# Matrix operands of a hybrid decoder layer moved by 64 bytes within on-chip memory

## The chip, the cores and the metric

The kernel runs on one core of one Trainium2 chip. The metric is device time in microseconds (us); lower is better. Three runs of the kernel before took 2049.73, 2051.74 and 2052.04 us, a median of 2051.74 us. The engines' names in the profile are PE (matrix multiplication; PEld is its separate row for loading weights), DVE (vector), ACT (scalar, with its activation functions), POOL and SP; the last two mostly start transfers.

## The reference

One decoder layer over 512 positions of width 2048, in float32. What matters here is its matrix products:

```python
proj = einsum('bsd,de->bse', h, w_in)          # 2048 -> 5120: q, k, v, xr, xg
o_attn = stick_breaking_attention(q, k, v)     # 8 heads of 128
hr = rg_lru(causal_depthwise_conv(xr), ...)    # gated linear recurrence, 1024 wide
mixed = concat([rmsnorm(o_attn), rmsnorm(hr * gelu(xg))])
x = x + gt1 * einsum('bse,ed->bsd', mixed, w_out)       # 2048 -> 2048
hid = square(relu(einsum('bsd,df->bsf', h2, w_mlp_in))) # 2048 -> 8192
x = x + gt2 * einsum('bsf,fd->bsd', hid, w_mlp_out)     # 8192 -> 2048
```

Each sub-layer's input is normalised and then scaled and shifted by vectors that come from `c @ w_ada` (2048 -> 12288); the result is normalised once more.

## The kernel before, in words

Everything is kept transposed: 128 features on the partitions, positions along the row. A float32 operand is split into a high part of the format `float32r` and a low part that holds the rest, and each product is three matmuls: high weights times high data, high weights times low data, low weights times high data (`mm3`, lines 258 to 263, and lines 1099 to 1101). In a matmul the *weights* (128 x 128, 512 bytes of a partition) are loaded into PE by an instruction of their own, LDWEIGHTS, and the *moving operand* (256 or 512 columns, 1024 or 2048 bytes of a partition) is streamed past them.

- Up to about 670 us: the products with `w_in` and most of those with `w_out`. They are matmuls of 512 columns. The weights arrive by transfer in a tile `wr`, ACT copies the high part to `wh` (line 244) and DVE subtracts to get the low part `wl` (line 122). For the value projection (`v_mm`, lines 470 to 472) the roles are changed: the data are the weights, and 256 columns of `wh` and `wl` are the moving operand. The first product, up to 110 us, keeps its split weights in tiles `a`. Attention, the recurrence and the modulation vectors run beside these as background work, fed in by lanes that are advanced step by step (`tick`).
- From about 670 us to the end: the rest of `w_out` and the two MLP products, all with matmuls of 256 columns. The MLP is a Strassen-Winograd scheme: one step (`strassen`, 1080) is seven products of three matmuls, for two halves, so 42 matmuls. Its weights are combined by `operands` (lines 1050 to 1073): tiles `raw` and `ts`, split into `w3`, `w4` and, for every fifth one, `w5`. The moving operands, data of the first product and the squared hidden layer of the second, are in tiles `a`.

The order of the instructions on each engine comes from a scheduler that goes by priorities; the change touches neither priorities nor instructions.

What matters for the change is where tiles lie within a partition. There are two stacks. The left one grows upward; it holds small constants, then a tile `pad` that nothing reads, and after it `cb` (2 x 4096 bytes), `n` (5 x 2048), `a` (64 x 2048), and on top a stage: first `front` (`wr`, `wh`, `wl`, 2048 bytes each), later in the same place `mlp` (`w5`, 4096, and `w3`, 6 x 3072). The right one grows downward from the end of the memory; it holds a few vectors that fill 512 bytes, then the stage `rows` (`x`, `tt`) and later `sums` (`ts`, `raw`, `w4`). All of these sizes are multiples of 512 bytes, except the constants and the pad:

```python
const(PAD, "pad")
cb = [T("cb"), T("cb")]
for tag in ("n", "a"):
    new(tag)
stage("rows")
stage("front")
```

The constants end at byte 19808 of a partition. With a pad of 40 columns of 4 bytes, `cb` begins at 19968 = 39 x 512, so everything after it begins at 0 modulo 512. The end of the memory, 229376, is 448 x 512, so the tiles on the right are at 0 modulo 512 as well. A moving operand or a block of weights starts at a multiple of 512 bytes within its tile, so before the change both operands of every matmul that counts are at 0 modulo 512 bytes.

Of the kernel before, what the change touches and what calls it, by code (L numbers as in the profile page):

```python
# [40 lines left out]

URGENT = 150
EVAC = 88
PAD = 40

BUFS = {"cb": 2, "a": 64, "ga": 4, "n": 5}
COLS = {
    "wr": 512, "wh": 512, "wl": 512, "x": 1024, "cb": 1024, "tt": 1280, "n": 512, "a": 512, "ga": 4,  # L50
    "raw": 1024, "ts": 1024, "w3": 768, "w4": 1024, "w5": 1024,
}
STAGES = {
    "front": ("left", {"wr": 4, "wh": 3, "wl": 3}),
    "rows": ("right", {"x": 4, "tt": 4}),
    "sums": ("right", {"ts": 2, "raw": 3, "w4": 4}),
    "mlp": ("left", {"w5": 1, "w3": 6}),
}
BANKS = ["mm"] * 4 + ["z"] * 3 + ["o"]
BANKS2 = ["o"] + ["z"] * 3 + ["mm"] * 4  # L60
# [4 lines left out]
def hybrid_layer_kernel(  # L65
# [32 lines left out]
    def T(tag, dt=F32, cols=None):  # L98
        return new(next(split_tag) if tag == "w4" else tag, dt, cols)

    def new(tag, dt=F32, cols=None):
        count[0] += 1
        pool, bufs = (sp, BUFS[tag]) if tag in BUFS else pools[tag][:2]
        return pool.tile([P, cols or COLS[tag]], dt, tag=tag, name=f"{tag}_{count[0]}", bufs=bufs)
# [5 lines left out]
    def const(cols, name, dt=F32):  # L110
        return sp.tile([P, cols], dt, tag=name, name=name)
# [27 lines left out]
    new("ga")  # L139
    const(PAD, "pad")  # L140
    cb = [T("cb"), T("cb")]
# [1318 lines left out]
```

## Time and profile before

| | |
|---|---|
| median of three runs | 2051.74 us |
| the profiled execution's own time, and its span | 2051.77 us, 2050.1 us |
| PE busy | 2009.6 us, 14532 matmuls |
| weight loads (PEld) busy | 1904.8 us, 14532 loads |
| DVE busy | 1764.0 us |
| ACT busy | 1077.8 us |
| POOL busy | 181.0 us |
| transfers | 441.45 MB, 215 GB/s over the span |

The rows of the profile name an engine, a line of the code, what is written and read (`ps_mm<-a,w`: a result bank from tiles `a` and `w3`, `w4` or `w5`, whose numbers are left out) and the shape. The ends of matmuls are modelled and overlap the next one, so what a matmul costs in a row of them is read from the distance between two starts, which the text calls the pitch, and not from its duration.

### The profile page before, as it was taken

To read this page: it belongs to the slowest core of one execution; us is meant where nothing else is said; L and a number is where in the kernel's file an instruction comes from. 1 tells how busy PE (TensorE), PEld (TensorE's weight loads), DVE (VectorE), ACT (ScalarE), POOL (GpSimd) and SP (SyncE) were. 2 spreads that over 40 slices of the span, in tenths; PEclk is the share of its full clock that TensorE was granted. 3 is DMA by queue.
4 is the path that set the end of the run, shared out by engine and by line. 5 is a ranking of instruction groups with operands and counts; after the bars stand their busy time and mean duration, and the time that the engine had idled before them with its cause. 6 is when DMAs were issued, how large, how long until landed. Compare 5 with 4: busy or idle time off the path is not lost.

```text
span 2050.1 us, 37927 instructions
## 1 busy us (share of the span) xinstructions
PE 2009.6 (98%) x14532; PEld 1904.8 (93%) x14532; DVE 1764.0 (86%) x2971; ACT 1077.8 (53%) x1572; POOL 181.0 (9%) x283
## 2 busy tenths in 40 slices
PE   8999999999999998999999999999999999999997
PEld 6789898778887998999999999999999999999996
DVE  8998776978888699999999999999788778778986
ACT  5443655796423575555555555456455555545542
POOL 0000000000000001221121112100011110210000
PEclk9999999999999999999999999999999999999998
DMA  9896646556789444675566656655485576667644
GB/s 363 303 326 201 200 153 203 167 172 206 226 300 325 134 156 149 213 238 182 185 217 198 194 188 220 211 191 176 148 308 207 210 254 235 232 241 248 237 148 149
DMA packets 205624, 441.45 MB, mean 215 GB/s; under 512 B 20353, under 2 KB 41985, under 8 KB 205442
## 3 DMA queue, kind: packets, MB, share of 16 engines
q1 hardware_dynamic: 178642, 360.78, 53.7%
q0 software_dynamic: 21760, 71.32, 8.9%
q10 hardware_dynamic: 5040, 6.93, 1.0%
q8 instruction: 114, 1.87, 0.4%
q14 instruction: 68, 0.56, 0.1%
HBM read 375.25 MB, written 63.70 MB: 214 GB/s over the span
## 4 chain that ended last, share of the span: by engine, by line
PE 57%; DVE 2%; DMA 1%; issue 0%; ACT 0%; SPq 0%; DVEq 0%
PE ps_mm L1101 9%; PE ps_mm L1100 9%; PE ps_mm L1099 9%; PE ps_z L1101 7%; PE ps_z L1100 7%; PE ps_z L1099 7%; PE ps_o L1101 2%; PE ps_o L1099 2%; PE ps_o L1100 2%; DMA raw<-in_w_mlp_out_dram 1%; DMA a<-x 0%; DVE w L122 0%; DMA a<-sum 0%; DVE a L1346 0%; DVE a L1276 0%
## 5 line engine op out<-in xcount | busy, mean ns | idle before, releaser
L1101 PE MATMUL ps_mm<-a,w 128*128 128x256 f32 x1696 | 479.6, 283 | 1.1 <-DVE w L122 1.1
L1100 PE MATMUL ps_mm<-a,w 128*128 128x256 f32 x1696 | 479.8, 283 | 0.0
L1099 PE MATMUL ps_mm<-a,w 128*128 128x256 f32 x1696 | 479.2, 283 | 0.0
L1063 ACT ACTIVATE w<-raw 128x768 fp32r<-128x768 f32 x244 | 204.9, 840 | 379.0 <-PE ps_mm L1100 165.6
L122 DVE TENSOR_TENSOR w<-ts,w 128x1024 fp32r<-128x1024 f32 x244 | 298.0, 1221 | 116.9 <-PE ps_mm L1100 61.6
L1101 PE MATMUL ps_z<-a,w 128*128 128x256 f32 x1304 | 369.5, 284 | 6.2 <-DVE w L122 6.2
L1099 PE MATMUL ps_z<-a,w 128*128 128x256 f32 x1304 | 369.3, 284 | 0.0
L1100 PE MATMUL ps_z<-a,w 128*128 128x256 f32 x1304 | 369.2, 284 | 0.0
L1101 PEld LDWEIGHTS ps_mm<-a,w 128*128 128x128 f32 x1696 | 325.5, 192 | 1.4 <-DVE w L122 1.4
L1100 PEld LDWEIGHTS ps_mm<-a,w 128*128 128x128 f32 x1696 | 325.7, 192 | 0.2 <-DVE a L122 0.2
L1099 PEld LDWEIGHTS ps_mm<-a,w 128*128 128x128 f32 x1696 | 325.5, 192 | 0.1
L1069 ACT ACTIVATE w<-ts 128x1024 fp32r<-128x1024 f32 x244 | 258.2, 1058 | 113.4 <-DVE ts L1065 101.9
L122 DVE TENSOR_TENSOR w<-raw,w 128x768 fp32r<-128x768 f32 (+1 forms) x296 | 267.4, 904 | 34.3 <-ACT w L244 23.4
L1101 PEld LDWEIGHTS ps_z<-a,w 128*128 128x128 f32 x1304 | 250.6, 192 | 7.1 <-DVE w L122 7.0
L1099 PEld LDWEIGHTS ps_z<-a,w 128*128 128x128 f32 x1304 | 250.8, 192 | 0.1
L1100 PEld LDWEIGHTS ps_z<-a,w 128*128 128x128 f32 x1304 | 250.7, 192 | 0.1
L244 ACT ACTIVATE wh<-wr 128x512 fp32r<-128x512 f32 (+1 forms) x184 | 113.0, 618 | 152.2 <-PE ps_mm L262 65.8
L259 PE MATMUL ps_mm<-a,wh 128*128 128x512 f32 x448 | 176.2, 393 | 3.1 <-ACT wh L244 1.4
L263 PE MATMUL ps_mm<-a,wl 128*128 128x512 f32 x448 | 175.1, 391 | 0.4 <-DVE wl L122 0.2
L262 PE MATMUL ps_mm<-a,wh 128*128 128x512 f32 x448 | 174.7, 390 | 0.0
L1057 DVE TENSOR_TENSOR ts<-raw 128x512 f32<-128x512 f32 x244 | 166.6, 683 | 3.5 <-DMA raw<-in_w_mlp_out_dram 2.4
L122 DVE TENSOR_TENSOR wl<-wr,wh 128x512 fp32r<-128x512 f32 (+1 forms) x184 | 123.7, 675 | 33.3 <-ACT wh L244 32.8
(332 smaller groups left out, 4167.0 us busy)
## 6 DMA issues: line engine op xcount, KB each, us to landing
raw<-in_w_mlp_out_dram SPq DMA_DIRECT2D x124, 512.0 KB, 4.0
raw<-in_w_mlp_in_dram SPq DMA_DIRECT2D x120, 512.0 KB, 3.9
x<-in_w_adaT_dram SPq DMA_DIRECT2D x108, 512.0 KB, 5.7
wr<-in_w_in_dram SPq DMA_DIRECT2D x160, 256.0 KB, 3.4
tt<-in_w_adaT_dram SPq DMA_DIRECT2D x52, 512.0 KB, 6.5
part<-a POOLq DMA_DIRECT2D x84, 256.0 KB, 3.9
a<-part SPq DMA_DIRECT2D x84, 256.0 KB, 6.0
prod<-a POOLq DMA_DIRECT2D x63, 256.0 KB, 5.9
```

Source lines behind the costliest of these rows:

```text
L122: tt(out=out, in0=full, in1=f32(high), op=ALU.subtract)
L244: act(h[:, :n], r[:, :n], AF.Copy)
L259: first = mm(out, wh, ah, start=start, stop=False, **kw)
L262: mm(out, wh, al, start=False, stop=False, **kw)
L263: mm(out, wl, ah, start=False, stop=stop, **kw)
L1057: tt(out=t[:, : 2 * HT].rearrange("p (a b) -> p a b", a=2), in0=r[:, HT : 3 * HT].rearrange("p (a b) -> p a b", a=2), in1=r[:, q_(0)].unsq ...
L1063: act(h, r[:, HT:], AF.Copy)
L1069: act(h, t, AF.Copy)
L1099: mm(out, wh[:, blk(i)], ah, start=st, stop=False, **kw)
L1100: mm(out, wh[:, blk(i)], al, start=False, stop=False, **kw)
L1101: mm(out, wl[:, blk(i)], ah, start=False, stop=j == js[-1], **kw)
```

## The change

The pad becomes 16 columns (64 bytes) smaller, and a tile of 64 bytes is put in front of the stage `mlp`:

```diff
-PAD = 40
+PAD, SHIFT = 24, 16
...
-    "raw": 1024, "ts": 1024, "w3": 768, "w4": 1024, "w5": 1024,
+    "raw": 1024, "ts": 1024, "w3": 768, "w4": 1024, "w5": 1024, "shift": SHIFT,
 }
 STAGES = {
     "front": ("left", {"wr": 4, "wh": 3, "wl": 3}),
     "rows": ("right", {"x": 4, "tt": 4}),
     "sums": ("right", {"ts": 2, "raw": 3, "w4": 4}),
-    "mlp": ("left", {"w5": 1, "w3": 6}),
+    "mlp": ("left", {"shift": 1, "w5": 1, "w3": 6}),
```

`cb`, `n`, `a`, `wr`, `wh` and `wl` now begin 64 bytes lower, at 448 modulo 512. `w5` and `w3` are where they were, and so is everything on the right (`x`, `tt`, `ts`, `raw`, `w4`): 0 modulo 512. So the matmuls of 512 columns have both operands at 448, the matmuls of 256 columns from 670 us on have the moving operand at 448 and the weights at 0, and `v_mm` has both at 448. No instruction is added, removed or changed but for these addresses.

## The prediction

> **What bounds the kernel now.** I read the page's first two parts, then the table by stage, then the groups of matmuls, then single starts in the timeline. The top of the page:
>
> ```profile
> span 2050.1 us, 37927 instructions
> PE 2009.6 (98%) x14532; PEld 1904.8 (93%) x14532; DVE 1764.0 (86%) x2971; ACT 1077.8 (53%) x1572; POOL 181.0 (9%) x283
> PEclk9999999999999999999999999999999999999998
> DMA  9896646556789444675566656655485576667644
> ```
>
> PE works 98% of the span at the full granted clock, so the kernel is as long as its matmuls take. Whether another engine would take over at once is read from the table by stage (PE, PEld, DVE, ACT, POOL, then clock, DMA share and GB/s):
>
> ```profile
> 0.00:110.00 110.00, 98.16 (x401) 77.58 (x402) 100.35 (x192) 51.89 (x86) 5.59 (x9) 0.98 0.92 337
> 110.00:260.00 150.00, 149.26 (x884) 132.83 (x883) 128.30 (x212) 71.59 (x114) 0.00 (x0) 1.00 0.69 231
> 671.00:800.00 129.00, 123.47 (x1002) 122.19 (x1001) 108.31 (x219) 83.16 (x162) 7.74 (x14) 0.99 0.44 136
> 800.00:1300.00 500.00, 499.00 (x4155) 498.56 (x4154) 476.26 (x820) 265.63 (x349) 86.36 (x127) 1.00 0.63 205
> 1390.00:2000.00 610.00, 608.50 (x5060) 607.54 (x5060) 498.80 (x746) 314.91 (x415) 60.64 (x112) 1.00 0.63 219
> ```
>
> From 800 to 1300 us DVE is busy for 476 of 500 us, so PE could gain there at most 24 us before DVE bounds it; from 1390 to 2000 us DVE has 111 us of room. The first 110 us hang on transfers and DVE, not on PE.
>
> **What a matmul costs now.** Of 256 columns, and of 512 (starts in the left column):
>
> ```profile
> 1099.75 0.28 PE L1099 MATMUL ps_mm<-a,w 128*128 128x256 f32 x1
> ...
> 1100.95 0.28 PE L1100 MATMUL ps_mm<-a,w 128*128 128x256 f32 x1
> 549.71 0.39 PE L259 MATMUL ps_mm<-a,wh 128*128 128x512 f32 x1
> ...
> 550.84 0.39 PE L263 MATMUL ps_mm<-a,wl 128*128 128x512 f32 x1
> ```
>
> Ten pitches of the first in 1.20 us make 0.120 us; five of the second in 1.13 us make 0.226 us. In one place the clock was granted at half:
>
> ```profile
> 390.52:392.93 2.41, 2.40 (x10) 0.56 0.72 232
> 392.93:393.89 0.96, 0.96 (x4) 0.50 0.48 169
> 392.83 0.31 PE L652 MATMUL ps_z<-tt,nones_r 128*128 128x128 f32 x1
> 392.94 0.73 PE L259 MATMUL ps_z<-a,a 128*128 128x512 f32 x1
> 393.47 0.63 PE L262 MATMUL ps_z<-a,a 128*128 128x512 f32 x1
> 393.90 0.54 PE L263 MATMUL ps_z<-a,a 128*128 128x512 f32 x1
> ```
>
> There 512 columns took 0.43 us (the last two starts) and 128 columns 0.11, a quarter: in proportion, with nothing on top. So at full clock the columns alone are 0.43/2 = 0.215 us for 512 and 0.107 for 256, and what is paid on top is 0.226 - 0.215 = 0.011 and 0.120 - 0.107 = 0.013 us: about the same for both sizes, once per matmul, and absent at half clock. A fixed number of PE's own cycles would have doubled there. So it looks like a time that the streamed operand loses while the next weights are read beside it. That is the one place in which addresses can count: two readers of one memory, whose start addresses are now equal modulo 512 everywhere.
>
> Two more readings say how much that loss can move. After a stall, when the load of weights and the stream stand otherwise to one another, the pitch is another for some matmuls, at the same addresses:
>
> ```profile
> 1380.48 0.28 PE L1100 MATMUL ps_z<-a,w 128*128 128x256 f32 x1
> ...
> 1381.43 0.28 PE L1099 MATMUL ps_z<-a,w 128*128 128x256 f32 x1
> 1941.81 0.28 PE L1099 MATMUL ps_o<-a,w 128*128 128x256 f32 x1
> ...
> 1942.74 0.28 PE L1101 MATMUL ps_z<-a,w 128*128 128x256 f32 x1
> 112.76 0.40 PE L259 MATMUL ps_mm<-a,wh 128*128 128x512 f32 x1
> ...
> 113.92 0.39 PE L263 MATMUL ps_mm<-a,wl 128*128 128x512 f32 x1
> ```
>
> Eight pitches of 256 columns took 0.95 us in the one place and 0.93 in the other: 0.1175 on the mean, 2 to 3 ns under the settled 0.120. Five pitches of 512 columns took 1.16: 0.232, 6 ns over the settled 0.226. So phase matters; the settled phase is a good one for 512 columns and a poor one for 256. The floor is set by the loads themselves; one behind the other, with no stream beside the first, they follow at 0.11 us:
>
> ```profile
> 1380.26 0.19 PEld L1099 LDWEIGHTS ps_z<-a,w 128*128 128x128 f32 x1
> 1380.37 0.19 PEld L1100 LDWEIGHTS ps_z<-a,w 128*128 128x128 f32 x1
> ```
>
> **The change part by part.** It adds and removes no instruction. The matmuls that it touches, by group (the groups of the other two lines of each product have the same counts):
>
> ```profile
> L1101 PE MATMUL ps_mm<-a,w 128*128 128x256 f32 x1696 | 479.6, 283 | 1.1 <-DVE w L122 1.1
> L1101 PE MATMUL ps_z<-a,w 128*128 128x256 f32 x1304 | 369.5, 284 | 6.2 <-DVE w L122 6.2
> L1101 PE MATMUL ps_o<-a,w 128*128 128x256 f32 x416 | 118.0, 284 | 0.4 <-DVE w L122 0.4
> L259 PE MATMUL ps_mm<-a,w 128*128 128x256 f32 x168 | 48.3, 287 | 0.7 <-DVE a L1324 0.4 <-ACT w L244 0.3
> L259 PE MATMUL ps_z<-a,w 128*128 128x256 f32 x92 | 26.2, 285 | 0.0
> L259 PE MATMUL ps_o<-a,w 128*128 128x256 f32 x44 | 12.6, 287 | 0.0
> L470 PE MATMUL ps_mm<-wh,a 128*128 128x256 f32 x128 | 36.5, 285 | 0.3 <-DVE a L460 0.3
> L259 PE MATMUL ps_mm<-a,wh 128*128 128x512 f32 x448 | 176.2, 393 | 3.1 <-ACT wh L244 1.4 <-DVE a L460 1.1 <-DVE a L481 0.6
> ```
>
> *256 columns, stream at 448, weights at 0.* (1696 + 1304 + 416) x 3 = 10248 in the MLP and (168 + 92 + 44) x 3 = 912 beside it: 11160 matmuls. Only here does the distance between the operands change, by 64 bytes. That is 16 columns, 16 x 0.107/256 = 6.7 ns of the stream: as large as the shifts that the stalls made (2 to 6 ns of pitch). No row shows this pair of addresses. Bounds: below, 0.111 us, the floor of the loads; above, the 6 ns by which 512 columns stand worse after a stall, 0.126. I take the nearest row, the pitch of 256 columns out of its settled phase, 0.118 (0.1175, rounded towards no gain): 11160 x 0.002 = 22 us less. DVE's cover holds: from 800 to 1300 us the 4155 matmuls give 8 us, and DVE's 476 us fit into 492.
>
> *512 columns, both at 448.* The distance stays zero, and the phase of the load against the stream with it. The settled 0.226 is the lowest that I see, so 0; bounds -0.002 and +0.006 for some 2200 matmuls, -4 to +13 us.
>
> *v_mm, both at 448*, some 770 matmuls: the distance stays; 0, with bounds of 2 ns each way, 1.5 us. In attention's last product the weights move and the stream (`tt`) does not, in the recurrence's gates too: under 150 matmuls, less than 1 us either way.
>
> *Vector and scalar work on moved tiles.* The convolution reads and writes at offsets of 4, 8 and 12 bytes:
>
> ```profile
> L554 DVE SCALAR_TENSOR_TENSOR a<-a,vec,a 128x510 f32<-128x510 f32 x8 | 5.9, 741 | 0.0
> L717 DVE SCALAR_TENSOR_TENSOR a<-a,vec,n 128x512 f32<-128x512 f32 x16 | 11.6, 742 | 0.0
> ```
>
> 741 ns at an odd offset, 742 without: 0 for DVE. ACT has no such pair of rows; 0 by the same, and with 315 of 610 us it has room for any small loss.
>
> *Transfers into `a`, `n` and `wr`.* No row shows one that starts off 512 bytes. Where they count is the first 110 us, at a DMA share of 0.92:
>
> ```profile
> wr<-in_w_in_dram SPq DMA_DIRECT2D x160, 256.0 KB, 3.4
> a<-in_xT_dram SPq DMA_DIRECT2D x16, 256.0 KB, 6.4
> ```
>
> Of these, 32 + 16 of 256 KB come there, 12.6 MB of the 37 MB that 337 GB/s make in 110 us. If they took a tenth longer, 0.34 x 0.1 x 110 = 4 us; it is zero if the addresses don't matter to a transfer. I take 0.5 us, near zero, since DVE is busy for 100 of the 110 us too. Later the share is 0.63 and loads run ahead: nothing. The Trainium skill (DMA: Bandwidth & Descriptors, "How a descriptor splits into AXI transactions") says that a transaction starts at a multiple of 256 bytes and that a descriptor starting elsewhere pays for bytes that it doesn't use; a row of 2048 bytes from 192 modulo 256 would by my estimate take 70 beats where it took 64, 9% more. It speaks against the change; no run yet shows it.
>
> *The tile of 64 bytes.* Each tile of `mlp` now lies over one tile of `front` more, so its first writer waits for one more old reader. That happens once, around 650 us, when eight blocks of weights in `w4` go first: 0.5 us, bounds 0 and 3.
>
> Sum: -22 + 0.5 + 0.5 = -21 us. The profiled execution's own time is 2051.77 us, the median of the runs 2051.74, the same within 0.03: 2031 us.
>
> **The rivals.**
>
> *Much faster.* The new distance takes the loss away altogether: 0.111 us per matmul of 256 columns. For it: at half clock the loss is nil, so it is no part of PE's own work. Against it: even the best phases after a stall lose most of it. Time: 5060 x 9 ns = 46 us from 1390 to 2000, 1002 x 9 = 9 from 671 to 800, DVE's 24 (not 37) from 800 to 1300, and 8 for the rest: 87 less, 1965 us.
>
> *No change.* The loss is the same at every address. While 512 bytes of weights are read, the stream runs through 1024, so it passes the weights' position once modulo 512 wherever it starts; what it loses in passing might not depend on where. For it: in all of the MLP, where tiles lie at many addresses, the pitch is 0.120, so nothing above 512 bytes matters. Against it: the pitches after stalls. Time: 2052 us.
> The Trainium skill (TensorE: Matmul & The Clock Gate, "Step-by-step: what each phase is for") also leads there: PE has two independent read ports, and loading weights takes nothing from the running matmul, so no address could matter. By its section "Back-to-back issue gap", 256 columns would take 256/2.4 + 2.5 = 109 ns; the trace has 120, so it disagrees in size, and the rule stays only a rival.
>
> *Slower.* The distance of 64 bytes puts stream and load into a worse settled phase, in the same 11160 matmuls. For it: 512 columns lose 6 ns more after a stall, so worse phases exist, and nothing in the trace says on which side this one lies. Against it: for 256 columns the phases seen are on the whole better than the settled one. Half of that price, 0.123, gives 11160 x 0.0028 = 31 us more, 2083 us; the whole, 0.126, gives 2118. It is slower from any settled pitch above 0.1204, the 4 us that a measurement of this kernel can tell from none (0.2%).
>
> **How the numbers follow.** Two of three places after a stall are better phases for their size, and they are the ones with 256 columns; so a better pitch is the likeliest. Chances: forecast 0.33, with its own range 2015 to 2047; much faster 0.20 (1960 to 2015); no change 0.20; slower 0.27 (2056 to 2118). Faster 0.53, same 0.20, slower 0.27. The range leaves out about 1 in 10 at each end, half of the much faster case and a third of the slower one: 1985 to 2085 us.
>
> **What would show it.** Right: about 850 matmuls in 100 us from 1100 us on, where 500 us now hold 4155; the pitch of 512 columns still 0.226; DVE at 97% from 800 to 1300. Wrong: a pitch of 256 columns at or over 0.120; a pitch of 512 columns that moves, which would mean that addresses count by themselves and not by their distance; or transfers into `wr` that land later than 3.4 us.

## The result and the profile after

The changed kernel took 2021.41 us (median of four runs, 2020.68 to 2022.22) where the kernel before took 2050.73: a ratio of 0.9858, interval 0.9841 to 0.9876. It is 29 us faster; the forecast was 2031. That these four agree so well seems to be chance: the same kernel, run again, took from 2014.53 to 2034.26 us (experiment 6, which also says why).

The profiled execution took 2022.22 us, with this page and this table by stage (PE, PEld, DVE, ACT, POOL, clock, DMA share, GB/s):

```profile
span 2020.5 us, 37927 instructions
PE 1967.8 (97%) x14532; PEld 1857.3 (92%) x14532; DVE 1761.0 (87%) x2971; ACT 1076.0 (53%) x1572; POOL 181.1 (9%) x283
0.00:110.00 110.00, 98.15 (x398) 77.58 (x399) 99.72 (x192) 52.37 (x85) 5.70 (x9) 0.98 0.92 336
671.00:800.00 129.00, 121.12 (x998) 118.68 (x996) 108.26 (x219) 82.99 (x162) 7.40 (x13) 0.97 0.43 133
800.00:1300.00 500.00, 496.35 (x4313) 494.08 (x4314) 491.13 (x847) 275.92 (x366) 91.34 (x135) 1.00 0.65 211
1390.00:2000.00 610.00, 604.82 (x5129) 601.74 (x5128) 498.89 (x755) 315.41 (x424) 60.63 (x112) 1.00 0.63 221
```

The first 110 us are as before, and nothing is gained from 671 to 800. From 800 to 1300 us PE starts 4313 matmuls where it started 4155, and DVE has gone from 476 to 491 busy of 500 us. From 1390 to 2000 us there are 5129 instead of 5060, but that window now takes in part of the kernel's end, where PE has little to do. From 1400 to 1850 us, before and after:

```profile
1400.00:1850.00 450.00, 450.00 (x3750) 449.83 (x3748) 358.19 (x527) 229.35 (x300) 53.01 (x98) 1.00 0.64 227
1400.00:1850.00 450.00, 450.00 (x3823) 450.00 (x3822) 362.84 (x533) 232.23 (x302) 52.64 (x98) 1.00 0.66 233
```

These are 73 more in 450 us, about half of the gain per microsecond of the stage before. Starts in the timeline tell the two stages apart, the first product of the MLP and the second:

```profile
999.78 0.28 PE L1101 MATMUL ps_mm<-a,w 128*128 128x256 f32 x1
...
1000.68 0.28 PE L1100 MATMUL ps_o<-a,w 128*128 128x256 f32 x1
1599.77 0.28 PE L1099 MATMUL ps_mm<-a,w 128*128 128x256 f32 x1
...
1600.71 0.28 PE L1101 MATMUL ps_mm<-a,w 128*128 128x256 f32 x1
```

Eight pitches took 0.90 us in the first place and 0.94 in the second: about 0.113 and 0.118. Over long unbroken stretches the two are 0.1133 and 0.1178: the same instruction on the same addresses settles at one of two pitches, and stays there until PE next stalls. Counted over the starts of the 11160 matmuls of 256 columns (the MLP's 10248 and the 912 beside it), 5429 pitches were of 115 ns or less and 5590 of 116 to 125 ns, 4088 of these in one unbroken stretch from 1400 to 1882 us. Before, every settled stretch stood at 0.1200.

Where PE waited from 800 to 1380 us, before and after (us in total, times, longest):

```profile
PE ps_z L1101 <- DVE w L122: 0.6, 1, 0.6
PE ps_o L1101 <- DVE w L122: 0.4, 1, 0.4
```

```profile
PE ps_z L1099 <- ACT a L1110: 1.5, 1, 1.5
PE ps_z L1099 <- DVE a L1115: 1.1, 2, 0.6
PE ps_mm L1099 <- DVE a L1111: 1.1, 1, 1.1
PE ps_z L1101 <- DVE w L122: 0.8, 2, 0.6
```

The first is the whole of that view before, 1 us; after, these four and five smaller ones make 6 us. So the quicker PE now waits in this stage, most often for DVE; experiment 11 tests that it is DVE. The starts show more than this view: taking every pitch above 125 ns among the 11160 matmuls as a stall, what the stalls hold beyond 0.120 us each went from 16.3 to 33.5 us. Of that, 2.2 became 12.4 us between 800 and 1400 us, 8.8 became 13.3 before 800 us, which takes back what the pitch gained there, and 5.2 became 7.9 after 1400 us.

### The profile page after: what moved, and what is told of

The parts are those of the page before. It is cut to its first block, busy times and chain, and to the rows that moved or that the text cites. A ratio compares the mean times of both kernels' runs of the same rounds, so it can differ in the third digit from the quotient of the medians.

```text
span 2020.5 us, 37927 instructions
## 1 busy us (share of the span) xinstructions
PE 1967.8 (97%) x14532; PEld 1857.3 (92%) x14532; DVE 1761.0 (87%) x2971; ACT 1076.0 (53%) x1572; POOL 181.1 (9%) x283
## 5 line engine op out<-in xcount | busy, mean ns | idle before, releaser
L1101 PE MATMUL ps_mm<-a,w 128*128 128x256 f32 x1696 | 472.4, 279 | 1.6 <-DVE w L122 1.6
L1099 PE MATMUL ps_mm<-a,w 128*128 128x256 f32 x1696 | 472.0, 279 | 1.9 <-DVE a L1111 1.1
L1100 PE MATMUL ps_mm<-a,w 128*128 128x256 f32 x1696 | 472.3, 279 | 0.2 <-DVE a L122 0.2
L1101 PE MATMUL ps_z<-a,w 128*128 128x256 f32 x1304 | 364.8, 280 | 7.5 <-DVE w L122 7.5
L1099 PE MATMUL ps_z<-a,w 128*128 128x256 f32 x1304 | 364.6, 280 | 3.1 <-ACT a L1110 1.5
L1100 PE MATMUL ps_z<-a,w 128*128 128x256 f32 x1304 | 364.0, 279 | 0.1
L1099 PEld LDWEIGHTS ps_mm<-a,w 128*128 128x128 f32 x1696 | 321.5, 190 | 2.5 <-issue 2.0
L1101 PEld LDWEIGHTS ps_mm<-a,w 128*128 128x128 f32 x1696 | 318.8, 188 | 2.1 <-DVE w L122 2.0
L1100 PEld LDWEIGHTS ps_mm<-a,w 128*128 128x128 f32 x1696 | 318.6, 188 | 0.6 <-DVE a L122 0.6
L1101 PEld LDWEIGHTS ps_z<-a,w 128*128 128x128 f32 x1304 | 246.0, 189 | 9.2 <-DVE w L122 9.1
L1099 PEld LDWEIGHTS ps_z<-a,w 128*128 128x128 f32 x1304 | 248.0, 190 | 4.5 <-ACT a L1110 1.7
L1100 PEld LDWEIGHTS ps_z<-a,w 128*128 128x128 f32 x1304 | 245.7, 188 | 0.6 <-DVE a L122 0.6
L211 DVE SCALAR_TENSOR_TENSOR x<-x,cb 128x1024 f32<-128x1024 f32 x108 | 131.1, 1217 | 29.5 <-DMA x<-in_w_adaT_dram 29.3
```

Source lines behind the costliest of these rows:

```text
L211: ins = stt(out=t, in0=t, scalar=1.0, in1=cb[q_], op0=ALU.mult, op1=ALU.mult, accum_out=self.ga[:, q_ : q_ + 1],)
L1099: mm(out, wh[:, blk(i)], ah, start=st, stop=False, **kw)
L1100: mm(out, wh[:, blk(i)], al, start=False, stop=False, **kw)
L1101: mm(out, wl[:, blk(i)], ah, start=False, stop=j == js[-1], **kw)
```

## The experiments

Theory: the distance between the two operands' addresses sets the pitch. Rivals: the moving operand's own address sets it; or the wait before a run of matmuls does, and the addresses little. The second question became why the time of one kernel varies, and the third what DVE takes back.

**1. micro.** PE alone: sets of 36 and 24 matmuls of the same kind and order, moving operand and weights at chosen offsets, each set begun after a wait of varied length. It computes nothing of the layer.

```diff
+for rep in range(4):
+    for m, w in N256:          # offsets in bytes, (moving, weights)
+        run(256, m, w, 36, rep)
```

> Not the layer: only PE is measured. Sets of 36 matmuls of 256 columns (24 of 512) in the order of the layer's triples, a short wait between sets, each set with other start addresses modulo 512 (moving operand, weights); four rounds with waits of other lengths (three for 512). Theory 1, the distance of the two operands counts: (0,0), (64,64), (256,256) and (448,448) all settle at 0.120 us; (448,0) and (0,64) both settle at 0.1133 or 0.1178, as in the changed kernel; 512 columns settle at 0.2267 for (0,0) and (448,448), and at another pitch for (448,0). Theory 2, the moving operand's own address counts: (448,448) goes with (448,0), and (0,64) with (0,0). No theory says which other distance is best; the floor of the loads, 0.111, bounds them.

Merged rows of the timeline: pitch is the duration less one matmul's 0.28 us (0.39 for 512 columns), over the count less one. In this order: (0, 0), (448, 448), (448, 0), (0, 64), (64, 0), and for 512 columns (0, 0) and (448, 0).

```profile
118.39 1.72 PE L67 MATMUL b<-mv,wt 128*128 128x256 f32 x13
188.68 1.60 PE L67 MATMUL b<-mv,wt 128*128 128x256 f32 x12
173.83 1.64 PE L67 MATMUL b<-mv,wt 128*128 128x256 f32 x13
203.82 1.75 PE L67 MATMUL b<-mv,wt 128*128 128x256 f32 x14
133.24 1.81 PE L67 MATMUL b<-mv,wt 128*128 128x256 f32 x14
483.78 1.75 PE L67 MATMUL b<-mv,wt 128*128 128x512 f32 x7
527.65 1.79 PE L67 MATMUL b<-mv,wt 128*128 128x512 f32 x7
```

The first is 1.44/12 = 0.120, the second 1.32/11 = 0.120, the third 1.36/12 = 0.1133, the fourth 1.47/13 = 0.113, the fifth 1.53/13 = 0.118. Equal offsets gave 0.120 wherever both lay (0, 64, 256, 448), and so did (256, 0) and (0, 256), and for 512 columns 64, 128 and 192 gave the pitches of 320, 384 and 448: the pattern repeats after 256 bytes. (0, 64), with nothing at 448 but the same distance, gave 0.1133 in three of four rounds and 0.1178 in one. For 512 columns distance 0 is the best, 1.36/6 = 0.2267, and (448, 0) worse, 1.40/6 = 0.2333. So the theory stands against the moving operand's own address. One pair of addresses can take either of two pitches, in rounds that differ in the wait before a set.

**2. all448.** The whole right stack 64 bytes lower as well, so nearly every operand is at 448.

```diff
-    "mlp": ("left", {"w5": 1, "w3": 6}),      # as before, but with PAD = 24
+    top.tile([P, SHIFT], F32, tag="rshift", name="rshift")   # on the right, 64 bytes
```

> The changed kernel with the weights of the 256-column matmuls at 448 too (no tile before w5 and w3, and the right stack 64 bytes lower), so both operands of nearly every matmul are moved by the same 64 bytes. Theory 1, the distance counts: the pitch of 256 columns is 0.120 again, 836 matmuls from 1100 to 1200 us, and the time that of before, 2051 us within 4. Theory 2, the moving operand's own address counts: the pitch stays at 0.113 to 0.118 and the time at 2021 us.

2052.42 us (2050.30 to 2055.14, ten runs), ratio 1.0009, interval 1.0000 to 1.0019. The windows 800 to 1300 and 1400 to 1850 us:

```profile
800.00:1300.00 500.00, 499.53 (x4161) 499.29 (x4161) 477.15 (x821) 266.58 (x350) 86.57 (x127) 1.00 0.64 205
1400.00:1850.00 450.00, 450.00 (x3749) 449.85 (x3748) 357.94 (x527) 229.78 (x300) 53.15 (x98) 1.00 0.64 227
```

4161 matmuls against 4155 before: 448 by itself is worth nothing. The gain is the distance.

**3. front0.** The 64-byte tile ahead of the stage `front`: for matmuls of 512 columns the weights are at 0 and the moving operand at 448.

```diff
-    "front": ("left", {"wr": 4, "wh": 3, "wl": 3}),
+    "front": ("left", {"shift": 1, "wr": 4, "wh": 3, "wl": 3}),
```

> The changed kernel with wr, wh and wl back at 0 (a tile of 64 bytes before them as well), so that the 512-column matmuls have their moving operand at 448 and their weights at 0, but for the first product. Theory 1, the distance counts: their pitch leaves 0.2267 us; the gates, the only ones of 512 columns whose distance the change did alter (64 the other way), went up to 0.232, so slower is likelier: 1800 matmuls by 0 to 6 ns, 2021 to 2032 us. Theory 2, the moving operand's own address counts: as after, 2021 us.

2027.32 us, from 2018.08, 2019.40, 2035.31 and 2035.24; ratio 0.9886, interval 0.9841 to 0.9932. First the changed kernel's row, then that of this one:

```profile
500.00:600.00 100.00, 99.54 (x438) 81.83 (x437) 93.50 (x164) 44.68 (x74) 4.74 (x2) 1.00 0.73 238
```

```profile
500.00:600.00 100.00, 100.00 (x428) 80.05 (x427) 92.97 (x162) 44.08 (x73) 4.14 (x1) 1.00 0.72 234
800.00:1300.00 500.00, 497.60 (x4223) 495.59 (x4221) 483.76 (x830) 272.73 (x360) 88.17 (x129) 1.00 0.64 206
1400.00:1850.00 450.00, 449.83 (x3965) 449.40 (x3964) 377.67 (x557) 240.52 (x316) 53.13 (x98) 1.00 0.67 237
```

The distance does make 512 columns slower, 428 against 438 in 100 us (by their starts 0.2333 against 0.2267 us). But from 110 to 672 us PE waited some 4 us less for other engines, and `v_mm`, whose operands are now 64 bytes apart, went from 0.120 to 0.118. The MLP's first matmul starts at 767.2 us where it started at 765.2, and in experiment 6 the unchanged kernel starts it at 767.2 as well, so no loss in all can be told. The times fall into two pairs 17 us apart. The profiled run (2018.08) has its two MLP stages the other way round from the changed kernel's: 450/3965 = 0.1135 in the second and 500/4223 = 0.118 in the first. 4088 matmuls times 4.4 ns, the two pitches' difference, are 18 us. So the pairs fit a second stage that fell into the one pitch or the other; no run of the slower pair was profiled.

**4. gt2_after.** The changed kernel with less vector work in the MLP's first stage: 64 products of the last modulation vector cover 8 of their 512 columns. It leaves out the rest of that vector. The same cut serves in 8, 9 and 11.

```diff
-                out=t, in0=t, scalar=1.0, in1=cb[q // 2][:, q % 2 * S : (q % 2 + 1) * S], ...
+                out=t[:, :8], in0=t[:, :8], scalar=1.0, in1=cb[q // 2][:, q % 2 * S : q % 2 * S + 8], ...
```

> The changed kernel, with the 64 vector products for the last modulation vector done on 8 of their 512 columns (the rest is left out; transfers and order stay): DVE has some 33 us less to do between 850 and 1400 us. Theory: in that stretch DVE, busy for 491 of 500 us, has become the bound, and the stalls that PE now has there go away: 8 to 18 us faster than after, 2003 to 2013 us. Rival: the stalls come from transfers or from the choice of settled pitch alone: 2021 us within 4.

2012.12 us, from 2012.76, 2011.47, 2033.19 and 2008.24; ratio 0.9840, interval 0.9779 to 0.9902. Its profiled run had 4230 matmuls from 800 to 1300 us, so the stage stood at 0.118; experiment 6 had 4219 there at the same pitch and with all of the vector work, so at 0.118 the cut is worth little. For the time as a whole the run is inconclusive: the draw of the pitch hides the effect.

**5. micro2.** As micro, with every distance in steps of 8 bytes and eight rounds. It computes nothing of the layer.

```diff
-N256 = [(m, 0) for m in (0, 16, 32, 64, 96, 128, 192, ...)] + ...
+N256 = [(m, 0) for m in range(0, 256, 8)] + [(0, w) for w in (16, 32, 48, 64, 80)]
```

> Only PE is measured, as in micro: sets of 27 matmuls of 256 columns (18 of 512), now at every distance of 8 bytes from 0 to 248 (16 for 512), since micro showed that what holds at 64, 128 or 192 holds 256 bytes on as well; eight rounds with waits of other lengths between the sets. Five sets have the distance on the weights' side. Theory: which of two settled pitches a set falls into (0.1133 or 0.1178 at 448, as in the changed kernel) is decided by the wait before it, so a distance of 192 shows both among eight rounds, and the weights at 64 likewise. Open, and what this run is for: whether some distance settles at 0.1133 or lower in all eight rounds, which would give a kernel that doesn't depend on it. Rival: the pitch hangs on the distance alone, and the two values in the kernel come from something else (other engines, transfers): then each distance has one pitch in all eight rounds.

(192, 0) in two rounds, (112, 0), (240, 0) and (0, 16):

```profile
259.42 1.58 PE L65 MATMUL b<-mv,wt 128*128 128x256 f32 x12
998.96 1.64 PE L65 MATMUL b<-mv,wt 128*128 128x256 f32 x13
219.54 1.64 PE L65 MATMUL b<-mv,wt 128*128 128x256 f32 x13
283.24 1.68 PE L65 MATMUL b<-mv,wt 128*128 128x256 f32 x13
291.17 1.71 PE L65 MATMUL b<-mv,wt 128*128 128x256 f32 x13
```

The first two rows are one pair of addresses: 1.30/11 = 0.118 and 1.36/12 = 0.1133, the higher in seven rounds, the lower in one. (112, 0) stood at 0.1133 in all eight. The last two have the same distance and differ, 1.40/12 = 0.1167 and 1.43/12 = 0.119. Their pitches go round in a short cycle, which these rows cut off; over whole cycles the starts give 0.1171 and 0.1183 in every round. So below 32 bytes the distance isn't everything. For 512 columns (0, 0) settled at 0.2267 in both rounds, (240, 0) ran at 0.2267 in one round and 0.2333 in the other, and the rest lay from 0.229 to 0.234, some of them with two pitches as well.

**6. after_again.** The changed kernel once more, unchanged.

> The changed kernel itself, once more. Theory: from 1400 to 1880 us no wait interrupts the matmuls, and the wait before 1400 decides by a hair whether those 4088 settle at 0.1133 or 0.1178 us, so its times fall into two groups 18 us apart, or all into one of them: 2021 or 2003 us. Rival, the pitch is fixed by the kernel: all its times at 2021 us within 2.

2026.69 us, from 2034.26, 2024.20, 2014.53 and 2029.17; ratio 0.9876, interval 0.9848 to 0.9904. The profiled run, the slowest:

```profile
800.00:1300.00 500.00, 497.39 (x4219) 495.60 (x4219) 483.72 (x828) 272.21 (x360) 87.87 (x129) 1.00 0.64 206
1400.00:1850.00 450.00, 450.00 (x3819) 449.67 (x3818) 364.37 (x537) 234.30 (x306) 53.00 (x98) 1.00 0.66 233
```

500/4219 and 450/3819 are both 0.118, where the first profiled run had its first stage mostly at 0.1133. Instead of the two groups that I expected, the times spread over 20 us: the first stage is a draw too. The ratio of the result holds for its four runs; this kernel's time is 2014 to 2034 us.

**7. d112.** A distance of 112 bytes through the weights: moving operand at 384, MLP weights 16 bytes higher.

```diff
-PAD, SHIFT = 24, 16
+PAD, SHIFT = 8, 32
+BY = 16          # added to the addresses of w3, w4, w5 and three small vectors
```

> The changed kernel with the moving operand of 256 columns 112 bytes ahead of the weights modulo 256 (cb, n, a, wr, wh, wl at 384, the weights in w3, w4, w5 at 16 modulo 512; the mask of attention moves into the stage front to make room), a distance at which all eight sets measured alone settled at 0.1133 us. Theory: all of the MLP settles at 0.1133; from 1400 to 1880 us that is 4088 x 4.4 ns = 18 us less than after, and some 900 matmuls between 800 and 1300 us give 4 less what DVE takes back there: 1998 to 2005 us, and the times agree among themselves. Rival: in the layer, with other engines at work, this distance has two settled pitches as well: two groups of times, or 2021 us.

2051.20 us (2042.55 to 2053.54, twelve runs), ratio 0.9999, interval 0.9989 to 1.0009.

```profile
800.00:1300.00 500.00, 499.29 (x4154) 498.60 (x4153) 476.29 (x818) 266.03 (x348) 87.90 (x129) 1.00 0.63 204
1400.00:1850.00 450.00, 450.00 (x3799) 449.80 (x3799) 363.40 (x536) 233.78 (x307) 53.00 (x98) 1.00 0.65 229
```

0.120 in the first stage, 0.1185 in the second: the expectation failed. The distance is micro2's, but there the odd 16 bytes were the moving operand's, here the weights'. The theory, that the distance alone counts, held wherever both offsets were multiples of 64 bytes, and falls with an odd 16.

**8. d112_gt2.** The same with the cut of experiment 4.

> d112 with the 64 vector products for the last modulation vector done on 8 of 512 columns (the rest left out), some 33 us less work for DVE between 850 and 1400 us. With one settled pitch, this tells what DVE costs there. Theory: at 0.1133 us the matmuls of that stretch need 472 us for what took 500, DVE needs 476, so DVE is the bound in parts of it: 5 to 12 us faster than d112. Rival: the stalls come from transfers or waits at the ends of the groups: within 3 us of d112.

2043.94 us (2034.12 to 2055.00, ten runs), ratio 0.9977, interval 0.9957 to 0.9998. That is 7 us under d112, in number as expected, but the times spread over 21 us and the profiled run (2053.16) stood at 0.120 in both stages. It tells nothing of DVE as a bound at 0.1133, since its pitch isn't 0.1133.

**9. gt2_before.** The kernel before with that cut.

> The kernel before, with the same 64 vector products cut to 8 columns. Theory: at 0.120 us PE is the bound and DVE, at 95%, has just room: 2050 us within 3. Rival: DVE held up PE before as well: 2040 us or less.

2050.50 us (2047.10 to 2053.45, ten runs), ratio 0.9999, interval 0.9990 to 1.0008. At 0.120 that vector work costs nothing: DVE was no bound before.

**10. d112m.** The 16 bytes on the moving side, as in micro2: `cb`, `n`, `a` and the front's weights at 368 modulo 512 (112 modulo 256), the MLP's weights at 0.

```diff
-PAD, SHIFT = 24, 16
+SHIFT, BY = 40, 16          # no pad; BY is added to the addresses of cb, n, a, wr, wh, wl
-    const(PAD, "pad")
```

> d112 moved the weights to 16 modulo 32 bytes, micro2 the moving operand; micro2 also showed that below 32 bytes the distance is not all: (240,0) settled at 0.1168, (0,16), the same distance, at 0.1182. Here, on the changed kernel, the moving side (cb, n, a, wr, wh, wl) is at 368 modulo 512 and the weights in w3, w4, w5 stay at 0: the very pair of micro2's distance 112, where eight of eight sets settled at 0.1133. Theory: all of the MLP at 0.1133 us, 875 matmuls or more per 100 us from 1400 to 1850 us, times that agree among themselves at 1998 to 2008 us, unless transfers into rows that start off 32 bytes are slower. Rival: in the layer other engines or transfers decide the settled pitch: two groups of times, or a pitch at or over 0.1178.

2006.86 us (2003.89 to 2009.57, five runs), ratio 0.9788, interval 0.9774 to 0.9801: better than both kernels, and the runs agree.

```profile
500.00:600.00 100.00, 99.88 (x429) 80.27 (x429) 93.33 (x164) 43.97 (x73) 4.13 (x1) 1.00 0.72 237
800.00:1300.00 500.00, 494.57 (x4310) 490.76 (x4309) 491.08 (x844) 275.78 (x366) 91.25 (x134) 1.00 0.65 211
1400.00:1850.00 450.00, 450.00 (x3971) 450.00 (x3971) 374.27 (x552) 240.42 (x318) 58.11 (x107) 1.00 0.68 242
```

450/3971 = 0.1133 through the whole window, and five runs lie within 6 us: the draw is gone. The first stage holds 4310, not the 4412 that 0.1133 would give, and its waits name DVE first:

```profile
PE ps_z L1098 <- DVE a L1114: 2.1, 4, 0.6
PE ps_z L1098 <- ACT a L1109: 1.3, 1, 1.3
PE ps_mm L1098 <- DVE a L1110: 1.1, 1, 1.1
```

The front pays for it: 429 matmuls of 512 columns per 100 us against 438, though both operands moved together there. By their starts they run at 0.232 and not at 0.2267, and `v_mm`, with both operands at 112 modulo 256 too, at 0.1176 and not at 0.120. So equal addresses are not one case either, once they are off 32 bytes.

**11. d112m_gt2.** The same with the cut.

> d112m with the 64 vector products for the last modulation vector done on 8 of 512 columns (the rest left out). All of the MLP now settles at 0.1133 us, so this tells what DVE costs there: it is busy for 491 of 500 us from 800 to 1300 us, and PE has some 16 us of waits among the matmuls of that product, against 4 before. Theory: DVE is the bound in parts of that stretch, and with 33 us less of its work most of those waits go: 5 to 13 us faster than d112m, 1994 to 2002 us. Rival: the waits come at the ends of the groups, where results are combined, whatever else DVE has to do: 2007 us within 3.

1995.53 us (1990.63 to 1999.31, five runs), ratio 0.9731, interval 0.9713 to 0.9749.

```profile
800.00:1300.00 500.00, 498.85 (x4389) 497.87 (x4388) 474.61 (x864) 280.50 (x369) 94.29 (x139) 1.00 0.68 217
```

79 more matmuls in the 500 us, times 0.1133, are 9 of the 11 us gained. Counted by starts as above, the stalls from 800 to 1400 us are 5.2 us where d112m has 16.1, which is nearly the whole gain. The cut that was worth nothing at 0.120 is worth 11 us at 0.1133: here DVE bounds parts of the first stage.

## Why the prediction was right, point by point

- **What is lost on each matmul** (a loss of the streamed operand beside the loading of weights, which addresses can change): held. Equal addresses at multiples of 64 bytes give 0.120 wherever they lie (micro, all448), and a distance of 64 bytes takes 2 to 7 ns off.
- **The distance, not the place**: held for the changed kernel (micro, all448); as a rule for any offset it is too simple (micro2, d112).
- **256 columns, 0.118 times 11160, 22 us**: right in sign, too small in size. The pitch was 0.1133 or 0.1178, the first below any row that I had taken a value from. Added up over the starts, the regular pitches became 48.1 us shorter. The sign of the pitch was argued from passing phases after stalls, at equal addresses, which go back to 0.120. That the value taken from them, 0.118, is also one of the two settled pitches of the new pair is luck, as no row tied the two together. From 1100 to 1200 us there are 874 matmuls, where the prediction expected about 850.
- **DVE's cover holds**: held at the pitch I took, and not at the one that came. Of the room that I read, 24 us between 800 and 1300 us, 15 were used, 491 busy of 500, and the stalls among the 11160 matmuls rose by 17.3 us, 10 of them between 800 and 1400 us. 48.1 - 17.3 = 30.8, which is what the stretch from their first start to their last became shorter; the span became 29.6 shorter. So the forecast came near by luck, through two errors of opposite sign: a pitch too high and no new wait.
- **512 columns, 0**: held, 438 against 439 matmuls from 500 to 600 us. In the recurrence's gates, where the weights moved and the stream did not, the distance did change. Starts before and after:

```profile
346.49 0.39 PE L259 MATMUL ps_z<-x,wh 128*128 128x512 f32 x1
...
347.62 0.39 PE L263 MATMUL ps_z<-x,wl 128*128 128x512 f32 x1
```

```profile
419.38 0.40 PE L259 MATMUL ps_z<-x,wh 128*128 128x512 f32 x1
...
420.54 0.39 PE L263 MATMUL ps_z<-x,wl 128*128 128x512 f32 x1
```

  Five pitches took 1.13 and then 1.16 us, 0.226 and 0.232: some 5 ns more each, and on so few under 1 us, as forecast. PE alone gave 0.2289 for this pair, (0, 448); the gates come at most six at a time and don't settle.
- **v_mm, the vector work, the 64-byte tile**: held; v_mm's pitch stays 0.120, DVE's sum is 1761.0 us against 1764.0.
- **Transfers, 0.5 us**: held. The landing times after, and with rows at 368 (experiment 10, second fence):

```profile
wr<-in_w_in_dram SPq DMA_DIRECT2D x160, 256.0 KB, 3.5
a<-in_xT_dram SPq DMA_DIRECT2D x16, 256.0 KB, 6.4
```

```profile
wr<-in_w_in_dram SPq DMA_DIRECT2D x160, 256.0 KB, 3.4
a<-in_xT_dram SPq DMA_DIRECT2D x16, 256.0 KB, 6.5
```

  3.4 before, 3.5 and 3.4 with rows off 256 bytes, at a DMA share of 0.92 in both kernels. A landing later than 3.4 was named as a sign of being wrong, but gt2_before, with nothing moved, has 3.5 too. The 9% that I estimated from the Trainium skill (DMA: Bandwidth & Descriptors, "How a descriptor splits into AXI transactions") doesn't show in these landings. Something does show in the queue of POOL, which carries most transfers out of `a` (and some into `n`). Packets, bytes and share of the span before and after:

```profile
q0 software_dynamic: 21760, 71.32, 8.9%
q0 software_dynamic: 21760, 71.32, 9.5%
```

  By the packets' own times that is 182 and 191 us for the same bytes, 5% more. It was 181 in gt2_before and 187 to 192 in every other whole-layer run that has moved `a`. The big queue of SP did not grow (1102 and 1093 us). PE's list of waits names none of these transfers.
- **Much faster**: its mechanism was half of what happened. The floor that it named, 0.111, isn't reached, but 0.1133 is, and DVE limits the first stage, as it said. With the better pair (d112m) the time is 2006.86.
- **No change**: refuted by all448 beside the changed kernel. The rule of the Trainium skill behind it (TensorE: Matmul & The Clock Gate, "Step-by-step: what each phase is for"), by which loading weights takes no read bandwidth from the running matmul, doesn't fit the traces: one instruction takes 0.120 or 0.1133 us by nothing but its operands' addresses. The 109 ns in the prediction go by a formula that the Trainium skill (TensorE: Matmul & The Clock Gate, "Back-to-back issue gap") gives for a matmul in isolation and not for pairs of load and matmul, so their difference from the trace's 120 says nothing about the rule.
- **Slower**: not at this distance; but worse pairs exist, for 512 columns (front0, micro: 0.2333) and for 256: in micro2 (136, 0) settled at 0.123 in seven of eight rounds, and (104, 0) at 0.130 in two. So the better sign at 64 bytes was no matter of course. (The 31 us of this rival's sum take 0.0028 us each; 0.123 less 0.120 is 0.003, 33 us.)

Still open: why the pitch follows the two operands' addresses in this way; what at a stall chooses between two pitches (rounds with different waits gave different ones, but no length was scanned finely or repeated, so mere chance isn't excluded); and d112's own pair, which was never measured alone.

## What to carry to other kernels

Where matmuls with weights of their own follow one another without a gap, the addresses of weights and stream against each other, modulo 256 bytes, are a parameter to scan: measure PE alone over the pairs, several rounds each after different waits, and take a pair that has one pitch in every round. A pair that is good on the mean but has two pitches gives a kernel whose time is a draw; look at starts over long stretches before one believes four runs that agree. And a few ns off the bound engine ask for the next engine's room by stage: here 15 of DVE's 24 us were gone at once.

## What the runs showed of the hardware

- A matmul of 256 columns beside the loading of the next weights settles at 0.1200 us when both operands' addresses are equal modulo 256 bytes and multiples of 64, at 0.1133 or 0.1178 with the stream 64 bytes behind, and at 0.1133 in all eight rounds with the stream at 112 and the weights at 0 (micro, micro2). For 512 columns equality at such addresses is the best of what was measured: 0.2267, against up to 0.234.
- Which of two pitches a run of matmuls takes is decided at a stall, and then holds: 4088 matmuls in one stretch, worth 18 us. Once settled, no stretch of 60 or more without a stall changed its pitch, in any trace of the whole layer.
- Pairs of the same distance can differ once an address is no multiple of 32 bytes: (240, 0) 0.1171 and (0, 16) 0.1183; in d112m, with both operands at 112 modulo 256, 512 columns run at 0.232 and not at 0.2267, and 256 columns (`v_mm`) at 0.1176 and not at 0.120.
- With the rows of `a` off 256 bytes, the packets of POOL's queue took 191 us where they took 182 for the same bytes; those of SP's queue took no longer (1093 and 1102).
